# A weight sum by two chained transfers, and a residual sum by ScalarE copies and accumulating transfers

## The chip, the cores and the metric

The kernel runs on one core of one Trainium2 chip. The metric is the device time of one execution in microseconds. A core has five engines that each take their instructions in a fixed order: TensorE (PE; its weight loads are listed as PEld), VectorE (DVE), ScalarE (ACT), GpSimd (POOL) and SyncE (SP). SP issues most of the transfers (DMA), and POOL, too, can issue them.

## The reference

One encoder layer on x of 1024 tokens by 1024 columns, all in float32. An attention and retention part adds to x first. What matters here is the last part, the feed-forward one with 2816 hidden columns:

```
h2 = rmsnorm(x, norm2_w)
x = x + (silu(h2 @ w_gate) * (h2 @ w_up)) @ w_down
```

## The kernel before, in words

Every matrix product is made of three matmuls: each factor is split into a high part (rounded for PE) and a low part (what is missing), and high times high, high times low and low times high are summed in PSUM. For weights ACT writes the high part (`whi`) and DVE the low part (`wlo`); each of these two has two buffers in turn.

The tokens are worked in two halves of four blocks of 128. The first half's feed-forward part is plain. In the second half (`ffn_fast`) the gate and up products are made with 7 block products in place of 8 (a scheme after Winograd and Strassen). The hidden columns are worked in 11 pairs of 128-column tiles, and the pairs in groups: `self.groups` holds five groups of two pairs and a last one of one pair. For each pair the two weight matrices are cut in four quarters, q[0] to q[3], called quads: rows 0 to 511 or 512 to 1023 (c) and the first or second 128 columns of the pair (r). One quad holds the gate and the up part, 128 partitions by 1024 values. The seven weight factors m = 0 to 6 are made in `factor`:

- m = 0, 1 and 6 are q[0], q[1] and q[3] themselves
- m = 2 is s2 = s1 - q[0], with s1 = q[2] + q[3]; m = 3 is s1
- m = 4 is s3 = q[0] - q[2]; m = 5 is q[1] - s2, written over s2

The tiles s1, s2 and s3 take turns in a ring of two buffers (tag S), the quads in a ring of six. `chunk_parts` makes the high and low parts of two factors at a time; a pair of whi and wlo buffers holds two factors. `gate_up` runs PE over the seven products of a pair (24 matmuls each, 256 columns) and then the silu chain: ACT's tanh, three DVE instructions, ACT's write of the high part (Thi in the profile) and DVE's write of the low part (Tlo).

After a group's pairs comes `down`: for each of two column halves c of w_down (a chunk) and each of two pairs of token blocks, PE sums the products in two PSUM banks of 512 columns; six such banks take turns. DVE adds each bank to its residual tile `self.x1[b][c]`. In the last group the sum then goes to the output.

The tiles of tag wraw, three in turn, take the raw quarters of w_down and, ahead of this part, the normalised rows of x.

The order on each engine is set when the program is built. A planner in the kernel (`charge`, `tick`, `step`) estimates costs and due times and puts the preparation of later weights between matmuls; the build may then put an instruction ahead of earlier ones of its engine that are not ready yet by its own reckoning. In the profile nearly all instructions have line 99, that of the helper that records them, so groups are told apart by tile names: `S<-quad` is s1 or s3, `S<-S,quad` is s2, `S<-quad,S` is m = 5, `x<-d,x` a residual add, `u<-d` and `p<-d` are copies out of PSUM.

Of the kernel before, what the change touches and what calls it, by code (L numbers as in the profile page):

```python
# [10 lines left out]
AF = mybir.ActivationFunctionType  # L11
OP = mybir.AluOpType
# [3 lines left out]
S, D = 1024, 1024  # L16
# [6 lines left out]
NH = FFN // 128  # L23
# [95 lines left out]
class Layer:  # L119
# [14 lines left out]
    def new(self, pool, shape, dt, tag, bufs):  # L134

        t = pool.tile(shape, dt, tag=tag, name=tag, bufs=bufs)
        ring = self.rings.setdefault(tag, [])
        ring.append(t[:].tensor.name)
        if len(ring) > bufs:
            self.written[ring[-1]] = [(0, 1 << 30, self.touched.get(ring[-1 - bufs], 0.0), "")]  # L140
        return t
# [184 lines left out]
    def factor(self, pr, m):  # L326

        nc = self.nc
        q = self.quad(pr, 4)
        if m == 0:  # L330
            self.quad(pr + 1, 2)
        new = lambda: self.st([128, 2, 4, 128], tag="S", bufs=2)
        add = lambda out, a, b, op: nc.vector.tensor_tensor(out, a, b, op=op)
        if m == 2:
            self.s1, self.s2 = new(), new()
            add(self.s1, q[2], q[3], OP.add)
            add(self.s2, self.s1, q[0], OP.subtract)
            return self.s2
        if m == 3:
            return self.s1  # L340
        if m == 4:
            s3 = new()
            add(s3, q[0], q[2], OP.subtract)
            return s3
        if m == 5:
            add(self.s2, q[1], self.s2, OP.subtract)
            return self.s2
        return q[{0: 0, 1: 1, 6: 3}[m]]

    def chunk_parts(self, items):  # L350
        nc = self.nc
        hi, lo = [t[:, :1024 * len(items)].rearrange("p (i u k n) -> p i u k n", u=2, k=4, n=128) for t in self.wpair()]

        def fill():
            late = None
            for i, (pr, m) in enumerate(items):
                if late:
                    late()
                src = self.factor(pr, m)
                nc.scalar.activation(hi[:, i], src, AF.Copy)  # L360
                late = lambda i=i, src=src: nc.vector.tensor_tensor(lo[:, i], src, hi[:, i].bitcast(F32), op=OP.subtract)
                if m in (5, 6):
                    self.quad(pr + 1, m - 2)
                yield
            late()
        return (hi, lo), fill()
# [851 lines left out]
    def down(self, half, j0, g, hh, hl):  # L1218
        nc = self.nc
        for c in range(2):  # L1220
            hi, lo = self.weights()
            for t0 in (0, 2):
                ps = [self.pd(), self.pd()]
                for js in (range(g - 1), range(g - 1, g)):
                    for i in range(2):
                        ts = slice(128 * (t0 + i), 128 * (t0 + i) + 128)
                        for j in js:
                            nc.tensor.matmul(ps[i], hh[:, j, ts], hi[:, j, :], start=(j == 0), stop=False)
                            nc.tensor.matmul(ps[i], hh[:, j, ts], lo[:, j, :], start=False, stop=False)
                            nc.tensor.matmul(ps[i], hl[:, j, ts], hi[:, j, :], start=False, stop=(j == g - 1))  # L1230
                            self.tick()
                self.evacuate()
                for i in range(2):
                    b = 4 * half + t0 + i
                    xs = self.x1[b][c]
                    nc.vector.tensor_tensor(xs, ps[i], xs, op=OP.add)
                    if j0 == self.groups[-1][0]:
                        nc.scalar.dma_start(self.out[0, b * 128:(b + 1) * 128, 512 * c:512 * c + 512], xs)
# [115 lines left out]
```

## Time and profile before

| | us |
|---|---|
| median of 3 runs | 1301.08 |
| lowest and highest run | 1300.11, 1301.93 |
| the profiled execution | 1298.79 |
| its span | 1297.0 |
| PE busy in the span | 1258.3 |
| DVE busy | 1004.1 |
| ACT busy | 782.2 |
| POOL busy | 58.2 |

The span is what the profiler saw of the execution, from first to last instruction; the execution's own time has 1.79 us around it. An engine's busy time is the time in which it has an instruction under way. An idle time says nothing by itself: what counts is who waits for whom.

### The profile page before, as it was taken

What the parts mean: (1) busy time and instruction counts of PE and PEld (TensorE: products, weight loads), DVE (VectorE), ACT (ScalarE), POOL (GpSimd) and SP (SyncE); (2) the same over time, 40 slices, a digit from 0 to 9 for tenths busy, and PEclk for the clock granted to TensorE, in tenths of its full rate; (3) what the DMA queues carried; (4) which work ended last, traced back from release to release, by engine and by line L of the source; (5) the groups of instructions that cost most, each with busy time, mean ns of one, the idle gap of its engine ahead of it and who ended that gap; (6) DMA issues with size and microseconds to landing.
All of it is one profiled execution on the core that took longest, in us unless ns stands there. A gap on an engine that the chain in (4) does not pass through costs nothing.

```text
span 1297.0 us, 22620 instructions
## 1 busy us (share of the span) xinstructions
PE 1258.3 (97%) x8363; PEld 1131.0 (87%) x8363; DVE 1004.1 (77%) x2600; ACT 782.2 (60%) x1732; POOL 58.2 (4%) x68
## 2 busy tenths in 40 slices
PE   8799998999999999999999999999979999999998
PEld 7799898999999887888888878888969999898987
DVE  6679899888978877878787795645598787776866
ACT  7778976655695788468658944433355454443533
POOL 1401011010020000000000000000000000000000
PEclk8999999999999999999999999999989999999999
DMA  8433214221242222222223232225434242423311
GB/s 277 151 83 94 63 45 114 67 74 42 66 127 86 63 85 81 83 65 81 82 66 98 65 86 77 66 77 202 128 104 140 66 131 71 124 84 113 98 49 65
DMA packets 157790, 121.32 MB, mean 94 GB/s; under 512 B 8176, under 2 KB 137840, under 8 KB 157552
## 3 DMA queue, kind: packets, MB, share of 16 engines
q1 hardware_dynamic: 151744, 111.14, 29.1%
q10 hardware_dynamic: 5936, 8.74, 2.0%
q8 instruction: 65, 1.06, 0.3%
q14 instruction: 45, 0.37, 0.1%
HBM read 115.67 MB, written 4.19 MB: 92 GB/s over the span
## 4 chain that ended last, share of the span: by engine, by line
PE 70%; DVE 14%; ACT 10%; issue 3%; POOL 2%; DMA 1%; SPq 0%; ACTq 0%; POOLq 0%; DVEq 0%
PE d L99 60%; PE t L99 8%; ACT junk L99 4%; DVE wlo L99 2%; PE l L99 2%; DVE L L99 2%; ACT whi L99 2%; ACT Thi L99 1%; DMA bias<-in_near_dram 1%; DVE tr L99 0%; DVE cc L99 0%; DVE junk L99 0%; DVE maA L99 0%; DVE zqk L99 0%; POOL rc L99 0%
## 5 line engine op out<-in xcount | busy, mean ns | idle before, releaser
L99 PE MATMUL d<-whi,Thi 128*128 128x256 f32 (+2 forms) x1136 | 352.6, 311 | 5.5 <-ACT Thi L99 3.6
L99 PE MATMUL d<-wlo,Thi 128*128 128x256 f32 (+2 forms) x1136 | 342.7, 302 | 1.5 <-DVE wlo L99 1.4
L99 PE MATMUL d<-whi,Tlo 128*128 128x256 f32 (+2 forms) x1136 | 342.5, 302 | 0.0
L99 PEld LDWEIGHTS d<-whi,Thi 128*128 128x128 f32 x1136 | 216.0, 190 | 19.4 <-ACT Thi L99 5.9
L99 PEld LDWEIGHTS d<-wlo,Thi 128*128 128x128 f32 x1136 | 216.5, 191 | 10.3 <-DVE wlo L99 2.3
L99 PEld LDWEIGHTS d<-whi,Tlo 128*128 128x128 f32 x1136 | 215.9, 190 | 9.5 <-DVE Tlo L99 1.6
L99 ACT ACTIVATE whi<-wraw 128x512 fp32r<-128x512 f32 (+1 forms) x300 | 171.7, 616 | 69.4 <-PE d L99 55.5
L99 DVE TENSOR_TENSOR wlo<-wraw,whi 128x512 fp32r<-128x512 f32 (+1 forms) x302 | 197.3, 674 | 5.4 <-ACT whi L99 4.3
L99 ACT ACTIVATE junk<-sc,tc 128x384 bf16<-128x384 f32 (+5 forms) x186 | 163.6, 879 | 34.5 <-DVE tc L99 30.7
L99 PE MATMUL d<-Phi,whi 128*128 128x256 f32 x616 | 171.7, 279 | 8.1 <-ACT Phi L99 7.9
L99 PE MATMUL d<-Plo,whi 128*128 128x256 f32 x616 | 171.0, 278 | 0.0
L99 PE MATMUL d<-Phi,wlo 128*128 128x256 f32 x616 | 170.8, 277 | 0.0
L99 PE MATMUL d<-Thi,whi 128*128 128x512 f32 (+1 forms) x368 | 143.3, 390 | 0.0
L99 PE MATMUL d<-Tlo,whi 128*128 128x512 f32 (+1 forms) x368 | 141.9, 386 | 0.1
L99 PE MATMUL d<-Thi,wlo 128*128 128x512 f32 (+1 forms) x368 | 141.8, 385 | 0.0
L99 PEld LDWEIGHTS d<-Phi,whi 128*128 128x128 f32 x616 | 116.4, 189 | 9.2 <-ACT Phi L99 9.0
L99 PEld LDWEIGHTS d<-Plo,whi 128*128 128x128 f32 x616 | 116.2, 189 | 0.4 <-DVE Plo L99 0.2
L99 PEld LDWEIGHTS d<-Phi,wlo 128*128 128x128 f32 x616 | 116.2, 189 | 0.0
L99 DVE TENSOR_TENSOR x<-d,x 128x512 f32<-128x512 f32 (+1 forms) x64 | 39.1, 623 | 61.4 <-PE d L99 53.5
L99 ACT ACTIVATE whi<-S 128x1024 fp32r<-128x1024 f32 x44 | 45.4, 1054 | 67.6 <-PE d L99 57.3
L99 PEld LDWEIGHTS d<-Thi,wlo 128*128 128x128 f32 x368 | 69.1, 188 | 15.1
L99 PEld LDWEIGHTS d<-Tlo,whi 128*128 128x128 f32 x368 | 69.2, 188 | 12.7 <-DVE Tlo L99 0.4
(325 smaller groups left out, 2344.3 us busy)
## 6 DMA issues: line engine op xcount, KB each, us to landing
wraw<-in_w_down_dram SPq DMA_DIRECT2D x44, 512.0 KB, 3.8
wraw<-in_w_in_dram SPq DMA_DIRECT2D x24, 512.0 KB, 3.8
wraw<-in_w_gate_dram SPq DMA_DIRECT2D x44, 256.0 KB, 3.1
wraw<-in_w_up_dram SPq DMA_DIRECT2D x44, 256.0 KB, 3.5
quad<-in_w_gate_dram SPq DMA_DIRECT2D x44, 256.0 KB, 3.2
quad<-in_w_up_dram SPq DMA_DIRECT2D x44, 256.0 KB, 4.1
wraw<-in_w_in_dram SPq DMA_DIRECT2D x32, 256.0 KB, 3.4
wraw<-in_w_out_dram SPq DMA_DIRECT2D x16, 512.0 KB, 3.7
```

The costliest lines, as they stand in the source:

```text
L99: return f(*args, **kw)
```

## The change

Two parts, both in the second half.

First, DVE no longer makes s1. A new function `summed` loads q[2]'s rows and columns once more, straight into the tile of s1 (two transfers from SP, gate and up), and then has two transfers from POOL add q[3]'s rows and columns to it. For the first pair it is called when m = 0 is made, for a later one when m = 6 of the pair before is made. The quads are still loaded, since m = 4 and m = 6 use them.

Second, in `down` of the second half, in all groups but the last, ACT copies a bank to half of a tile of tag wraw, and a transfer from POOL adds that to the residual tile.

```
@@ factor @@
+        if (pr, m) == (0, 0):
+            self.summed(0)
         add = lambda out, a, b, op: nc.vector.tensor_tensor(out, a, b, op=op)
         if m == 2:
-            self.s1, self.s2 = new(), new()
-            add(self.s1, q[2], q[3], OP.add)
+            self.s1, self.s2 = self.s1, new()
             add(self.s2, self.s1, q[0], OP.subtract)
             return self.s2
...
+    def summed(self, pr):
+
+        if pr == NH // 2:
+            return
+        self.s1 = self.st([128, 2, 4, 128], tag="S", bufs=2)
+        for c, queue, kw in ((0, self.nc.sync, {}), (1, self.nc.gpsimd, {"accum_op": OP.add})):
+            for u, w in enumerate((self.w_gate, self.w_up)):
+                queue.dma_start(self.s1[:, u], w[512 * c:512 * c + 512, 256 * pr + 128:256 * pr + 256]
+                                .rearrange("(k p) n -> p k n", p=128), **kw)
...
@@ chunk_parts @@
                 if m in (5, 6):
                     self.quad(pr + 1, m - 2)
+                if m == 6:
+                    self.summed(pr + 1)
...
@@ down @@
                     xs = self.x1[b][c]
+                    if half and j0 < self.groups[-1][0]:
+                        if i == 0:
+                            tmp = self.sb([128, 1024], tag="wraw", bufs=3)
+                        ti = tmp[:, 512 * i:512 * i + 512]
+                        nc.scalar.activation(ti, ps[i], AF.Copy)
+                        nc.gpsimd.dma_start(xs, ti, accum_op=OP.add)
+                        continue
                     nc.vector.tensor_tensor(xs, ps[i], xs, op=OP.add)
```

## Rows read from the trace of the kernel before

**Rows 1.** The page's busy time of each engine, share of the span, instructions.
```profile
PE 1258.3 (97%) x8363; PEld 1131.0 (87%) x8363; DVE 1004.1 (77%) x2600; ACT 782.2 (60%) x1732; POOL 58.2 (4%) x68
```

**Rows 2.** Busy time of each engine (x instructions) in stretches, clock, DMA share, GB/s.
```profile
965.00:1280.00 315.00, 314.79 (x2251) 290.76 (x2251) 242.67 (x289) 146.89 (x207) 0.00 (x0) 1.00 0.31 91
...
1022.00:1032.00 10.00, 10.00 (x90) 10.00 (x89) 7.20 (x7) 5.70 (x7) 0.00 (x0) 1.00 0.59 158
1032.00:1042.00 10.00, 10.00 (x90) 10.00 (x89) 9.79 (x12) 5.94 (x8) 0.00 (x0) 1.00 0.29 84
```

**Rows 3.** Who waited for whom from 965 to 1280: total us, times, longest us.
```profile
ACT whi L99 <- PE d L99: 125.7, 41, 9.2
...
DVE S L99 <- DMA quad<-in_w_up_dram: 10.0, 5, 2.5
...
PEld d L99 <- ACT Thi L99: 1.8, 6, 0.7
PEld d L99 <- DVE Tlo L99: 1.6, 7, 0.3
...
PE d L99 <- ACT Thi L99: 0.2, 1, 0.2
```

**Rows 4.** The chain that ended last: start us, us, what.
```profile
961.51 149.28 PE d L99 x1102
...
1117.94 161.51 PE d L99 x1113
```

**Rows 5.** Stretches of 5 us ahead of 961, columns as in rows 2.
```profile
915.00:920.00 5.00, 5.00 (x45) 5.00 (x44) 0.84 (x2) 2.08 (x4) 0.00 (x0) 1.00 1.21 291
...
945.00:950.00 5.00, 0.00 (x0) 0.00 (x0) 5.00 (x10) 3.02 (x7) 0.00 (x0) 0.69 0.35 105
```

**Rows 6.** Timeline of DVE and SP: start us, us, instruction, [idle before <-releaser].
```profile
919.59 1.23 DVE L99 TENSOR_TENSOR S<-quad 128x1024 f32<-128x1024 f32 x1 [4.09 <-DMA quad<-in_w_up_dram]
...
917.57 1.11 SPq L99 DMA_DIRECT2D quad<-in_w_up_dram  x1
...
1022.47 0.50 SPq L99 DMA_DIRECT2D quad<-in_w_up_dram  x1
```

**Rows 7.** Groups by form from 965 to 1297: busy us, mean ns, idle before.
```profile
L99 DVE TENSOR_TENSOR x<-d,x 128x512 f32<-128x512 f32 x48 | 32.5, 691 | 47.5 <-PE d L99 47.4
...
L99 DVE TENSOR_TENSOR S<-quad 128x1024 f32<-128x1024 f32 x20 | 24.4, 1221 | 10.1 <-DMA quad<-in_w_up_dram 10.0
...
L99 ACT ACTIVATE u<-d 128x512 f32<-128x512 f32 x22 | 13.0, 590 | 8.1 <-PE d L99 8.1
```

**Rows 8.** Timeline of DVE in the second group, pairs 2 and 3.
```profile
1024.08 2.36 DVE L99 TENSOR_TENSOR wlo<-S,whi 128x1024 fp32r<-128x1024 f32 x2 [0.26 <-ACT whi L99]
...
1046.25 1.22 DVE L99 TENSOR_TENSOR wlo<-S,whi 128x1024 fp32r<-128x1024 f32 x1
...
1049.66 1.22 DVE L99 TENSOR_TENSOR S<-S,quad 128x1024 f32<-128x1024 f32 x1
...
1061.01 0.69 DVE L99 SCALAR_TENSOR_TENSOR Tlo<-th,Thi 128x512 fp32r<-128x512 f32 x1
```

**Rows 9.** Timeline of ACT, pairs 2 to 4.
```profile
1028.42 1.06 ACT L99 ACTIVATE whi<-quad 128x1024 fp32r<-128x1024 f32 x1 [2.06 <-PE d L99]
...
1033.82 1.06 ACT L99 ACTIVATE whi<-quad 128x1024 fp32r<-128x1024 f32 x1 [2.01 <-PE d L99]
...
1078.26 2.01 ACT L99 ACTIVATE whi<-S 128x1024 fp32r<-128x1024 f32 x2 [9.19 <-PE d L99]
```

**Rows 10.** Transfers: count, KB each, median us to landing; last line: all quads.
```profile
quad<-in_w_up_dram SPq DMA_DIRECT2D x44, 256.0 KB, 4.1
...
out_dram<-x ACTq DMA_DIRECT2D x8, 256.0 KB, 2.1
...
DMA to landing us min/median/max: 2.8/3.7/7.1
```

## The prediction

> **What bounds the kernel now.** I read the page's busy table first: TensorE (PE) is busy 97% of the span, VectorE (DVE) 77% [rows 1]. An average over stages says little about one stage, so next came the stretches. The change acts only from about 905 us on, in the feed-forward part of the second half. From 965 to 1280 us PE is busy 314.79 of 315.00 us, DVE 242.67, ScalarE (ACT) 146.89, GpSimd (POOL) 0.00 [rows 2]. Inside it, DVE is busy 9.79 of 10 us in one stretch and 7.20 in another; PE runs 90 matmuls in both [rows 2]. So a filled DVE does not slow PE here. The list of waits of the same stretch says what PE could get back: 1.8 + 1.6 + 0.2 = 3.6 us, all of it for Thi and Tlo, the hidden activations that the down products start on [rows 3]. ACT, by contrast, waits for PE 125.7 us [rows 3]. The chain that ended last agrees: its two long pieces are PE alone, 149.28 and 161.51 us [rows 4].
>
> Only ahead of 961 us does PE stand still for long: 0.00 busy in 945 to 950, where DVE is busy 5.00 of 5 [rows 5]. Nothing that the change removes is done there: the first s1 add runs at 919.59, and DVE had already waited 4.09 us for its transfer [rows 6].
>
> **The change, part by part.**
>
> *Removed.* Eleven s1 adds (half of the instructions S<-quad) at 1.22 us are 13.4 us. Of the 48 wide residual adds the last group keeps 8; 40 at 0.69 us are 27.6 us [rows 7]. DVE loses 41 us of work, yet PE can gain at most the 3.6 us above. I put 1.5 us: the Tlo part nearly whole, the Thi part not, since ACT writes Thi.
>
> *Copies on ACT.* 40 copies out of PSUM; the nearest row is u<-d, the same shape, 0.59 us [rows 7]: 23.6 us beside 146.89 busy in 315. Each can stand in ACT's queue behind a whi copy that waits for PE, 125.7 us in 41 waits [rows 3]. What waits for the copy is a PSUM bank; there are six, two for each pair of token blocks, so PE is two pairs ahead before it feels one. I take nothing; without that cover it is about one copy, 0.6 us, for each of ten weight chunks.
>
> *Residual transfers.* 40 SBUF to SBUF accumulations of 256 KB from POOL's queue. Nobody reads the sums until the next group's down stage, two pairs of 7 products later (37.8 us at the 2.70 us worked out below). The tmp tiles take turns in the wraw ring of three, so w_down loads of the next group come after those transfers; their values too are needed only at that stage. A load of the same bytes takes 4.1 us [rows 10]. Price: nothing; without the cover, one such landing a group.
>
> *The sum s1 by two transfers in a row.* This is the step that can cost. Two new SP loads stand in SP's queue behind the quads and ahead of the next quads and w_down loads; two accumulations wait for them on POOL, which does nothing else here [rows 2]. One issue takes SP about 0.5 us [rows 6], and what follows on SP is needed a pair later. But s1 takes the buffer of the previous pair's s2, free only when that pair's m = 5 low part is written. Take pair 3, the second of its group: that is at 1024.08 + 2.36 = 1026.44 [rows 8]. Then two issues, 1.0; a load, 4.1 (median of the up quarter [rows 10]); an accumulation. No accumulation is in the trace: below, 2.1 us (the landing of out<-x, the shortest median); above, 7.1 us (the slowest quad) [rows 10]; the nearest row is the up quarter, the same bytes from the same matrix, so 4.1. s1 is there at 1026.44 + 1.0 + 4.1 + 4.1 = 1035.6; with both legs short (2.8 + 2.1) at 1032.3, with both long (7.1 + 7.1) at 1041.6.
>
> When is it due? PE releases ACT's whi copies at 1028.42 and 1033.82 [rows 9]; a buffer holds two products, so a product takes 2.70 us. PE begins product (2,6) at 1033.8, (3,0) at 1036.5, (3,1) at 1039.2, (3,2) at 1041.9. Product (3,2) needs s2 (1.22), its whi (1.06) and its wlo (1.22) [rows 7 to 9]: s1 is due at 1041.9 - 3.5 = 1038.4. The margin is 2.8 us, and -3.2 with both legs long. That holds for the data of (3,2) alone. DVE takes its instructions in a fixed order: while s2 waits, wlo of (3,0) and (3,1) stand still if they are behind it.
>
> In the pairs that open a group s1 would land at 1046.25 + 1.22 + 9.2 = 1056.7 [rows 8] (bounds 1053.4 to 1062.7). Its reader, whi<-S at 1078.26 [rows 9], is 20 us off. But s2 stood at 1049.66, ahead of the silu instructions that end with Tlo at 1061.01 + 0.69 = 1061.70 [rows 8], and PE waits for Tlo in seven places already [rows 3]. If s2 keeps a place ahead of that Tlo, PE waits with it. If the order now puts it behind, that stretch is two adds, 2.4 us, shorter on DVE. I take one more short wait, of the 1.6 / 7 = 0.23 us that Tlo's average [rows 3], in each of five openings: 1.2 us, bounds 0 and those of the first rival.
>
> *A rule beside that row.* The rows give 4.1 us for each leg [rows 10]. The Trainium skill, page "DMA: Bandwidth & Descriptors", section "Anatomy of one DMA", fits one GpSimd-issued transfer as 2.0 us plus its bytes at 436 GB/s, an estimate of 2.6 us for 256 KB; by it s1 of pair 3 would stand at 1034.1. The same page, section "Two DMAs through the same engine are not ordered", has the second transfer wait for the first one's semaphore: the legs add up, as I have them, which no row here can show.
>
> *The first pair.* Its loads come behind twelve quad transfers, in a stretch with a transfer share of 1.21 [rows 5]. The last quad is issued at 917.57 and takes 1.11 us of SP [rows 6]; s1 stands at about 918.7 + 1.0 + 8.2 = 927.9. DVE has slack there (0.84 busy of 5 [rows 5]). I take 0.5 us, bounds 0 and 3.
>
> *Sum.* -1.5 + 1.2 + 0.5 = +0.2 us. The profiled execution took 1298.79 us (1.79 more than its span of 1297.0); the median of the runs, 1301.08, is 2.29 above it. So 1299.0 by the profile, 1301.3 for the median.
>
> **The rivals.** (1) *DVE stands still behind s2.* For it: DVE's order lets s1 wait for quads, 10.0 us in five places [rows 3], so it counts on transfers earlier than they land; two in a row double that error. Against: those five waits cost PE nothing. Place and price: in five group openings s2 stands ahead of Tlo, near 1054, and s1 lands at 1056.7: 2.7 us each, 13.5 us, 1314.6. With both legs long, 8.7 us there and 3.2 in five pairs inside groups, 59 us. It decides from the point where an accumulation takes over 1.4 us (1056.7 - 4.1 = 1052.6), if s2 has that place. (2) *PE gets faster.* As a mechanism: with DVE freer, matmuls follow one another closer, or the new order of DVE's queue gives back part of the 5 us at 945. Against the first: 90 matmuls in 10 us with DVE at 7.20 and at 9.79 [rows 2]. For the second only luck speaks; with 4 us of it the time is 1297. Beside this stands a rule: the Trainium skill, page "Trainium Kernel Development and Optimization", section "Best Practices", judges the distance to the roof by the busy share of weight loads, not of matmuls. Weight loads are busy 290.76 of 315 us [rows 2], so by that rule up to 24 us are open; the count of 90 does not bear it out. (3) *ACT's copies hold PSUM banks*: 0.6 us for each of ten chunks, 6 us, 1307; ACT's free half of the stretch speaks against it. (4) *DVE isn't relieved where it is full*: s2 waits longer than s1 took. Then the time is that of the forecast or of the first rival.
>
> **How the numbers follow.** The runs shown reach from 1300.11 to 1301.93, so 0.2%, 2.6 us, is about what can be told from no change. Forecast: 0.47, 1301.3, its own range 1299 to 1303.7. Rival 1: 0.39, mostly 1304 to 1320. Rival 2: 0.09. Rival 3: 0.05. Rival 4 is shared by the first two. Faster 0.09, same 0.47, slower 0.44. The range 1298.5 to 1319 leaves out some 0.07 at either end: below it rival 2, above it rival 1 with transfers nearer their upper bound.
>
> **What would show it.** Right: PE from 965 to 1280 still busy over 99.5%, with waits under 5 us; an accumulation landing within 5 us; DVE waiting at s2 for a transfer without PE waiting for wlo or Tlo; DVE's busy time in that stretch down by some 38 us, ACT's up by 23. Wrong: PE waits for wlo or Tlo of 1 us or more once in each group, with DVE at S<-S,quad before them; or PE waits for a bank after ACT's copies; or the stretch ahead of 961 is shorter or longer by more than 2 us.

## The result and the profile after

The changed kernel takes 1373.93 us (median of four runs, 1372.70 to 1377.18); the kernel before took 1301.07 us beside it. The ratio is 1.0568, 95% interval 1.0551 to 1.0585: 72.9 us slower. The forecast was 1301.3 us with a range up to 1319.0, so the result lies far outside. The nearest case is the first rival with long transfers (59 us), and the runs below show a second loss that no case of the prediction held.

The page of the changed kernel, busy time first (answers to [rows 1]), then TensorE's granted clock in 40 slices of the span:

```profile
PE 1286.0 (94%) x8363; PEld 1154.1 (84%) x8363; DVE 963.0 (70%) x2549; ACT 804.6 (59%) x1772; POOL 122.3 (9%) x130
...
PEclk9999999999999999999999999998899898999999
```

The relief is there as worked out: DVE 1004.1 to 963.0, 41.1 us less; ACT 22.4 us more. PE runs the same 8363 matmuls, is busy 27.7 us longer, and its share of the span falls. Where it stands still, the list of waits from 900 us on tells (us in total, times, longest):

```profile
DVE S L99 <- DMA S<-in_w_up_dram: 40.1, 5, 10.0
...
DVE S L99 <- issue: 27.1, 4, 10.0
PE d L99 <- ACT Thi L99: 21.6, 6, 5.5
PE d L99 <- DVE wlo L99: 21.4, 4, 6.0
```

In [rows 3] PE waited 3.6 us in all for Thi and Tlo. Now it waits 21.6 us for Thi and 21.4 for wlo, four to six times each, and DVE waits 67 us in nine places at S. Both waits of PE have one picture in DVE's timeline. First the second pair of a group, then the end of a group:

```profile
1039.57 2.35 DVE L99 TENSOR_TENSOR wlo<-S,whi 128x1024 fp32r<-128x1024 f32 x2
...
1047.76 0.68 DVE L99 TENSOR_TENSOR cc<-u,p 128x512 f32<-128x512 f32 x1
1058.47 1.23 DVE L99 TENSOR_TENSOR S<-S,quad 128x1024 f32<-128x1024 f32 x1 [10.04 <-DMA S<-in_w_up_dram]
...
1060.22 1.21 DVE L99 TENSOR_TENSOR wlo<-quad,whi 128x1024 fp32r<-128x1024 f32 x1
...
1085.24 1.23 DVE L99 TENSOR_TENSOR S<-S,quad 128x1024 f32<-128x1024 f32 x1 [5.70 <-issue]
1086.38 0.69 DVE L99 SCALAR_TENSOR_TENSOR th<-th,cc 128x512 f32<-128x512 f32 x1
...
1088.92 0.68 DVE L99 SCALAR_TENSOR_TENSOR Tlo<-th,Thi 128x512 fp32r<-128x512 f32 x1
```

S<-S,quad is s2. It stands in DVE's queue directly behind cc of the pair before, and DVE stands with it 10.04 us until the second transfer of s1 has landed. Behind it wait instructions that need nothing from it: the low part of product 1 (wlo<-quad, 1060.22) and, at a group's end, the tanh steps that lead to Thi and Tlo. (The releaser "issue" at 1085.24 says only that the trace shows none. It is the same instruction of another pair: the second transfer of its s1 was issued at 1077.10 and took 7.96 us to land, to 1085.06.) PE's timeline has the answer to both:

```profile
1055.16 0.28 PE L99 MATMUL d<-Plo,whi 128*128 128x256 f32 x1
1061.49 0.58 PE L99 MATMUL d<-Phi,wlo 128*128 128x256 f32 x1 [6.05 <-DVE wlo L99]
...
1082.64 0.39 PE L99 MATMUL d<-whi,Thi 128*128 128x512 f32 x1
1088.51 0.80 PE L99 MATMUL d<-whi,Thi 128*128 128x512 f32 x1 [5.48 <-ACT Thi L99]
```

The stand is not all that PE loses. Busy time by stretches (columns as in [rows 2]): the long stretch, then ahead of the pause, in it, just after it, and later:

```profile
965.00:1280.00 315.00, 275.48 (x1824) 252.62 (x1825) 166.65 (x196) 138.57 (x202) 48.84 (x48) 0.92 0.62 138
...
1050.00:1055.00 5.00, 5.00 (x46) 5.00 (x46) 0.00 (x0) 0.75 (x1) 2.62 (x2) 1.00 1.26 265
1056.00:1061.00 5.00, 0.00 (x0) 0.00 (x0) 2.52 (x3) 0.67 (x2) 0.00 (x0) 0.78 0.23 29
1061.50:1065.50 4.00, 4.00 (x19) 4.00 (x20) 4.00 (x6) 2.47 (x4) 0.00 (x0) 0.50 0.00 0
1066.00:1071.00 5.00, 4.48 (x38) 4.29 (x37) 5.00 (x7) 3.24 (x6) 0.00 (x0) 1.00 0.63 184
```

Ahead of the pause PE runs 46 matmuls in 5 us at a granted clock of 1.00 (2.4 GHz). In the pause the clock falls, and in the 4 us behind it 0.50 is granted (1.2 GHz): 19 matmuls where the earlier rate would give 37. The same 0.50 stands in the 4 us from 1088.55, 1213.85, 1240.95 and 1291.70, each behind another pause. So a pause is paid for again after it has ended.

The account, from the starts of PE's matmuls: the distance between two starts is 0.113 us for 256 columns and 0.2335 for 512 when nothing disturbs. An excess over 0.9 us counts as a pause, all others together as slow matmuls. It begins in both kernels with the 6002nd matmul (954.76 before, 958.99 after). Before: pauses 3.80, slow 4.03. After: pauses 49.25, slow 28.08, of which 23.4 lie within 8 us behind a pause. The differences are 45.45 us of pauses and 24.05 of slow matmuls. With the 4.23 us by which the 6002nd already starts later they make the 73.73 us by which the last one does (1292.89 and 1366.62).

The list of transfers (count, KB each, median us to landing) answers to [rows 10]:

```profile
quad<-in_w_up_dram SPq DMA_DIRECT2D x44, 256.0 KB, 5.0
...
S<-in_w_up_dram SPq DMA_DIRECT2D x11, 256.0 KB, 5.4
S<-in_w_gate_dram POOLq DMA_DIRECT2D x11, 256.0 KB, 4.7
S<-in_w_up_dram POOLq DMA_DIRECT2D x11, 256.0 KB, 6.8
```

The second leg of s1 lands after 6.8 us, not 4.1. And on SP's queue and POOL, around the pair above:

```profile
1001.96 40.10 SPq L99 DMA_DIRECT2D wraw<-in_w_down_dram  x4
...
1044.27 1.59 SPq L99 DMA_DIRECT2D S<-in_w_gate_dram  x1
...
1051.10 1.30 POOL L99 DMA_DIRECT2D S<-in_w_gate_dram  x1 [16.27 <-DMA S<-in_w_gate_dram]
1051.98 1.73 POOL L99 DMA_DIRECT2D S<-in_w_up_dram  x1
```

SP stands at four w_down loads for 40.10 us, to 1042.06. The loads of quads and of s1 are behind them. In [rows 6, 8] a quad of this pair was issued at 1022.47, ahead of the low parts at 1024.08; here the quads come after the same low parts (1039.57).

### The profile page after: what moved, and what is told of

Same layout as the page of the kernel before. It is cut to its first block, busy times and chain, and to the rows that moved or that the text cites. A ratio compares the mean times of both kernels' runs of the same rounds, so it can differ in the third digit from the quotient of the medians.

```text
span 1370.9 us, 22842 instructions
## 1 busy us (share of the span) xinstructions
PE 1286.0 (94%) x8363; PEld 1154.1 (84%) x8363; DVE 963.0 (70%) x2549; ACT 804.6 (59%) x1772; POOL 122.3 (9%) x130
## 5 line engine op out<-in xcount | busy, mean ns | idle before, releaser
L99 PE MATMUL d<-whi,Thi 128*128 128x256 f32 (+2 forms) x1136 | 356.4, 314 | 24.1 <-ACT Thi L99 21.6
L99 PE MATMUL d<-Phi,wlo 128*128 128x256 f32 x616 | 178.2, 289 | 21.4 <-DVE wlo L99 21.4
L99 PE MATMUL d<-Phi,whi 128*128 128x256 f32 x616 | 178.4, 290 | 11.3 <-ACT Phi L99 7.4
L99 PE MATMUL d<-Plo,whi 128*128 128x256 f32 x616 | 177.3, 288 | 0.0
L99 PEld LDWEIGHTS d<-Phi,wlo 128*128 128x128 f32 x616 | 122.4, 199 | 22.2 <-DVE wlo L99 22.2
L99 PEld LDWEIGHTS d<-Phi,whi 128*128 128x128 f32 x616 | 122.5, 199 | 13.7 <-ACT Phi L99 8.4
L99 PEld LDWEIGHTS d<-Plo,whi 128*128 128x128 f32 x616 | 122.0, 198 | 0.4 <-DVE Plo L99 0.2
L99 DVE TENSOR_TENSOR wlo<-S,whi 128x1024 fp32r<-128x1024 f32 x44 | 52.8, 1219 | 45.0 <-ACT whi L99 45.0
L99 DVE TENSOR_TENSOR wlo<-quad,whi 128x1024 fp32r<-128x1024 f32 x33 | 39.9, 1223 | 56.6 <-ACT whi L99 56.6
```

Of the source, the lines that this page charges most:

```text
L99: return f(*args, **kw)
```

## The experiments

Times are medians; the ratio is to the kernel before, run beside each, with its 95% interval. The first four put two questions: which part costs, and is it DVE's stand or the transfers.

**The sum alone** (residual adds left on DVE):

```diff
-                    if half and j0 < self.groups[-1][0]:
-                        ...
-                        nc.gpsimd.dma_start(xs, ti, accum_op=OP.add)
-                        continue
                     nc.vector.tensor_tensor(xs, ps[i], xs, op=OP.add)
```

> Only the weight sum by transfers; the residual stays with DVE adds. Theory W (DVE stands at s2 until the second transfer of s1 has landed, and everything behind it in DVE's queue with it): nearly all of the loss is here, 1350 to 1374 us, with a PE wait of 4 to 6 us in each pair from the second on. Rival Q (the tmp tiles hold up the w_down loads in SP's queue, and these hold up the quads and the loads of s1): without tmp tiles the loads are early, 1301 to 1320.

1365.33 us, ratio 1.0503 (1.0470 to 1.0535): 64 us. Waits, and the timeline of DVE and SP, of this kernel:

```profile
DVE S L99 <- DMA S<-in_w_up_dram: 27.5, 5, 6.1
...
PE d L99 <- ACT Thi L99: 19.6, 5, 5.0
DVE S L99 <- DMA wraw<-in_w_down_dram: 19.2, 4, 5.2
...
PE d L99 <- DVE wlo L99: 8.6, 4, 2.3
```

The third line names w_down, but it is s2 again: in all four places it starts 0.17 or 0.18 us after the second transfer of s1 has landed (at 1084.66 us and 1084.84, for one).

```profile
1042.75 2.36 DVE L99 TENSOR_TENSOR wlo<-S,whi 128x1024 fp32r<-128x1024 f32 x2 [0.26 <-ACT whi L99]
...
1044.01 0.37 SPq L99 DMA_DIRECT2D S<-in_w_gate_dram  x1
...
1057.52 1.23 DVE L99 TENSOR_TENSOR S<-S,quad 128x1024 f32<-128x1024 f32 x1 [6.06 <-DMA S<-in_w_up_dram]
```

The first load of s1 is issued at 1044.01, as soon as the first of the two low parts is written: that one frees the buffer. From there to s2 (1057.52) it is 13.5 us. The prediction had 9.2 for the same way, and counted from the second low part.

**The residual alone** (s1 added on DVE as before):

```diff
-        if (pr, m) == (0, 0):
-            self.summed(0)
...
-            self.s1, self.s2 = self.s1, new()
+            self.s1, self.s2 = new(), new()
+            add(self.s1, q[2], q[3], OP.add)
...
-                if m == 6:
-                    self.summed(pr + 1)
```

> Only the residual by ACT copies and accumulating transfers; s1 stays with DVE. Theory W: 1299 to 1304, no PE wait over 1 us after 962 us. Rival Q: the quads come late behind w_down loads, 1310 to 1340. Rival B (ACT copies hold PSUM banks): 1305 to 1310 with PE waits in the down stages.

1318.64 us, ratio 1.0137 (1.0114 to 1.0161): 17.4 us where I had priced nothing. What SP waited for most from 990 to 1300 us, then SP's queue and DVE, of this kernel:

```profile
SPq L99 <- DMA x<-wraw: 152.8, 18, 20.3
```

```profile
1011.97 14.91 SPq L99 DMA_DIRECT2D wraw<-in_w_down_dram  x3
...
1035.47 1.23 DVE L99 TENSOR_TENSOR S<-quad 128x1024 f32<-128x1024 f32 x1 [8.45 <-DMA quad<-in_w_up_dram]
```

The w_down loads take turns in the ring with the copies that ACT makes, so a load waits on SP for a copy's transfer (x<-wraw) to end, and the quads stand behind it. The kernel before has no such transfer. DVE waits 8.45 us at s1 where it waited 2.5 at most in [rows 3].

**The whole change, s2 made by GpSimd:**

```diff
-            add(self.s2, self.s1, q[0], OP.subtract)
+            nc.gpsimd.tensor_tensor(self.s2, self.s1, q[0], op=OP.subtract)
```

> The changed kernel, but s2 = s1 - q[0] is made by POOL in place of DVE, so that DVE never stands at it. Theory W: the waits for Thi at the group ends go (5 x 5.6 us and the slow clock after them), what stays is that the factor itself is late in the second pair of a group: 1315 to 1340. If DVE's standing is not the cause: 1365 to 1380.

1364.82 us, ratio 1.0477 (1.0460 to 1.0495). The expectation failed; the stand had moved to the next engine that takes its work in order:

```profile
ACT whi L99 <- POOL S L99: 41.6, 5, 10.1
PE d L99 <- ACT p L99: 37.6, 5, 9.3
```

ACT's copy whi of s2 now stands ahead of the copies p that free PE's banks. The run takes s2 off DVE, but not out of an in-order queue, and so does not tell place from lateness.

**The whole change, with one leg:** no accumulation; DVE adds the last quarter to s1.

```diff
+            add(self.s1, self.s1, q[3], OP.add)
...
-        for c, queue, kw in ((0, self.nc.sync, {}), (1, self.nc.gpsimd, {"accum_op": OP.add})):
+        for c, queue, kw in ((0, self.nc.sync, {}),):
```

> The changed kernel without the accumulating transfers of s1: q[2] is loaded into its tile by SP as in the change, and DVE adds q[3] to it before it makes s2. Theory W with the second leg as the main part (6 to 8 us from POOL's issue to its end): s1 stands about when the quads do, 1300 to 1312. If the first leg, behind the quads and after the wait for the ring, is already late: 1330 to 1360.

1339.72 us, ratio 1.0298 (1.0282 to 1.0313): the accumulation is worth 34 us of the 72.9, but not all.

**The residual with tiles of its own.** The copies go to tiles that hold PE's products (p1, u2, u3, p5) instead of the w_down ring; on top of the residual alone:

```diff
-                        if i == 0:
-                            tmp = self.sb([128, 1024], tag="wraw", bufs=3)
-                        ti = tmp[:, 512 * i:512 * i + 512]
+                        ti = self.st([128, 512], tag=("p1", "u2", "u3", "p5")[t0 + i])
```

> Only the residual part, with its copies in tiles that stand empty in the down stage (p1, u2, u3, p5) and not in the ring of the w_down loads. Theory Q (the 17 us of the residual part alone come from w_down loads that wait in SP's queue for those transfers, with quads behind them): the four PE waits of 2.5 to 4.2 us go, 1299 to 1303. If the accumulating transfers themselves or ACT's copies cost it: 1314 to 1320.

1301.96 us over 11 runs against 1300.37 over 15, ratio 1.0009 (1.0000 to 1.0018). Of 17.4 us 1.6 stay. SP and DVE of this kernel:

```profile
1000.19 2.77 SPq L99 DMA_DIRECT2D wraw<-in_w_down_dram  x2
...
1027.94 0.39 SPq L99 DMA_DIRECT2D quad<-in_w_up_dram  x1
...
1031.74 1.23 DVE L99 TENSOR_TENSOR S<-quad 128x1024 f32<-128x1024 f32 x1 [2.76 <-DMA quad<-in_w_up_dram]
```

The same 40 copies and 40 transfers, but SP is done with the w_down loads at 1002.96, 25 us ahead of the quad shown: the residual part's cost was the shared ring and SP's queue. It also tells what 27.6 us less on DVE are worth here when the copies and transfers that replace them add no wait: no time.

**The sum alone, first leg alone** (DVE adds the last quarter; no residual part): the edit of the one-leg run on the sum alone.

> Only the weight sum, and of it only the load of q[2] by SP; DVE adds q[3] and subtracts q[0]. Theory W with the second leg as the larger part of the 64 us: 1310 to 1325, DVE waiting 2 to 4 us for the load in each pair. If the first leg is as much: 1330 to 1345.

1325.02 us, ratio 1.0192 (1.0177 to 1.0207): 24.7 us. The second leg costs the other 40 of the sum's 64 us.

**A control, and an earlier start.** The control is the kernel before with five quad buffers instead of six. The second kernel is the sum alone; it has five too, gives s1 a buffer of its own, and calls the sum at product 4 instead of 6:

```diff
-            q = self.st([128, 2, 4, 128], tag="quad", bufs=6)
+            q = self.st([128, 2, 4, 128], tag="quad", bufs=5)
...
-        self.s1 = self.st([128, 2, 4, 128], tag="S", bufs=2)
+        self.s1 = self.st([128, 2, 4, 128], tag="S1", bufs=1)
...
-                if m == 6:
+                if m == 4:
                     self.summed(pr + 1)
```

> Control for the next run: the kernel before with five quad buffers in place of six. 1301 to 1310; quads come somewhat later. Both theories expect the same.

> Only the weight sum, with a buffer of its own for s1 (paid for with one quad buffer), called at m = 4 and so free after m = 3's low part: both transfers start some 6 us earlier and ahead of the next quads in SP's queue. Theory W (lateness of s1 is the whole cost): within 10 us of the control with five quads. If the transfers cost by their traffic or on POOL rather than by lateness: 1345 to 1370, as with the weight sum alone.

The control: 1311.98 us, ratio 1.0089 (1.0074 to 1.0105). The early start: 1349.44, ratio 1.0379 (1.0359 to 1.0399), 37.5 us over the control where I expected at most 10. DVE of the early start:

```profile
1043.73 1.23 DVE L99 TENSOR_TENSOR S<-S,quad 128x1024 f32<-128x1024 f32 x1 [4.72 <-issue]
1046.01 2.35 DVE L99 TENSOR_TENSOR wlo<-quad,whi 128x1024 fp32r<-128x1024 f32 x2
```

With s1 earlier, s2 has moved forward too, ahead of low parts that stood before it, and DVE again stands some 5 us. So my theory that s1 starts too late fell. What was left: s2 gets a place in DVE's queue a few us ahead of the landing, wherever the landing is.

**s2 fixed behind the low part of product 1.** One edge that orders two instructions on DVE; the edit touches no buffer and no transfer. On the sum alone:

```diff
-                late = lambda i=i, src=src: nc.vector.tensor_tensor(lo[:, i], src, hi[:, i].bitcast(F32), op=OP.subtract)
+                late = lambda i=i, src=src: setattr(self, "low", nc.vector.tensor_tensor(
+                    lo[:, i], src, hi[:, i].bitcast(F32), op=OP.subtract))
...
-            add(self.s2, self.s1, q[0], OP.subtract)
+            with self.tc.issue_after(self.low.ins):
+                add(self.s2, self.s1, q[0], OP.subtract)
```

> The sum part alone (residual adds on DVE as before), with one order fixed by hand: s2's subtraction may not stand in DVE's queue ahead of the low part of product 1 of its own pair. The transfers are untouched: same queues, same buffers, same starts. Theory P (the cost of the sum part is the place of s2 in DVE's in-order queue, some 5 us ahead of the landing of the accumulation, with the low part of product 1, the tanh steps and Tlo queued behind it): the waits of PE for Thi at the group ends (5.0 us each, about 20 us) and for the low part of product 1 (8.6 us) go, and most of the 28.8 us of slow matmuls with them; of the 64 us 15 to 60 go: 1305 to 1350, my value 1320, since in the middle of a group product 2 itself may still come 1 to 3 us late. Rival L (product 2 is late whatever stands ahead of it, since the accumulation lands too late for PE): PE waits as long, for the low part of product 2 in place of product 1's: 1355 to 1370. Rival T (the transfers themselves slow the rest): 1355 to 1370, with waits for quads or w_down loads.

1310.33 us, ratio 1.0066 (1.0052 to 1.0080): of 64 us 9 stay. The stretch of [rows 2], the waits, and DVE's timeline at a group's end and in the pair after it:

```profile
965.00:1280.00 315.00, 311.43 (x2183) 285.48 (x2182) 229.80 (x274) 142.45 (x202) 25.99 (x20) 1.00 0.52 125
```

```profile
DVE S L99 <- DMA S<-in_w_up_dram: 7.1, 5, 1.9
...
PE d L99 <- ACT p L99: 2.9, 4, 0.9
PE d L99 <- ACT Thi L99: 1.3, 1, 1.3
...
PE d L99 <- DVE wlo L99: 0.2, 1, 0.2
```

```profile
1075.26 1.22 DVE L99 TENSOR_TENSOR S<-S,quad 128x1024 f32<-128x1024 f32 x1
...
1100.40 1.23 DVE L99 TENSOR_TENSOR wlo<-quad,whi 128x1024 fp32r<-128x1024 f32 x1 [0.29 <-ACT whi L99]
1103.76 1.23 DVE L99 TENSOR_TENSOR S<-S,quad 128x1024 f32<-128x1024 f32 x1 [1.53 <-DMA S<-in_w_up_dram]
```

At the group's end s2 runs without a wait; inside the group it waits 1.53 us with the low part of product 1 already written, and PE is busy 311.43 of 315 us at a clock of 1.00. The transfers land as late: from the first load of s1 (1090.82) to s2 it is 12.9 us here, against 13.5 in the sum alone. What cost was the place of s2. Counted as in the account above, slow matmuls are 21.7 us more than before in the sum alone and 6.6 here.

**The same with the early start:**

> The kernel with the sum started at product 4 into a buffer of its own and five quad buffers (1349.4, against a control with five quad buffers at 1312.0), with the same order fixed: s2 behind the low part of product 1. Theory P: the two together leave nothing that is late; within 8 us of the control, 1304 to 1320. Rival L or T: most of the 37 us stays, 1335 to 1350.

1303.51 us (10 runs), ratio 1.0015 (1.0004 to 1.0027), and so below its control of 1.0089. In none of the eleven pairs does s2 wait for its transfers. Why it beats the control was not followed; five quad buffers made DVE wait for quads there, and this kernel's s1 needs no quads.

**The whole change with s2 fixed, and with both mends** (s2 fixed and the residual's own tiles):

> The whole change with s2 fixed behind the low part of product 1; the residual copies still take turns with the w_down loads. Theory P: the sum part's share falls away, and what stays is the residual part's 17 us through SP's queue: between 1315 and 1345. Rivals L and T: 1360 to 1375.

> The whole change with both mends: s2 behind the low part of product 1, and the residual copies in tiles of their own, so that no w_down load waits for them. Theory P with the finding on SP's queue: 1298 to 1325, at or a little above the result of the sum part alone with the same order, since the residual part in tiles of its own cost about 1 us. Not faster than the kernel before by more than 3 us, since PE computes without a gap there. Rivals L and T: 1350 to 1370.

1330.49 us, ratio 1.0218 (1.0202 to 1.0233), and 1309.25 us, ratio 1.0061 (1.0048 to 1.0074). The first of them, on SP and DVE:

```profile
1014.82 15.22 SPq L99 DMA_DIRECT2D wraw<-in_w_down_dram  x3
...
1046.42 1.23 DVE L99 TENSOR_TENSOR S<-S,quad 128x1024 f32<-128x1024 f32 x1 [6.28 <-DMA S<-in_w_up_dram]
```

Here the place is right and s1 itself comes late, behind SP's stand at w_down. The ring costs 21.2 us (1330.49 - 1309.25), as it cost 15.8 without the sum (17.4 - 1.6).

## Why the prediction was wrong, point by point

*"Residual transfers ... Price: nothing."* This step failed, with 17.4 us by itself. It asked when the values of w_down are needed, not what stands behind their loads on SP. The prediction itself says that the loads come after those transfers in a ring of three; the next line on that queue, the quads, is needed within a few us. Shown by the pair of runs that differ in the tiles alone (17.4 and 1.6 us).

*"If the order now puts it behind ... I take one more short wait ... in each of five openings: 1.2 us."* This step failed most. s2 kept a place ahead of the tanh steps, and PE stood at the groups' ends: 5.48 us in the one shown, 21.6 us for Thi in all. The first rival had this mechanism and both its places, openings and inner pairs; I gave it 0.39. Shown by the edge that moves s2 alone (64 to 9 us).

*The leg at 4.1 us.* Mis-sized: an accumulation takes 4.7 us for the gate half and 6.8 for the up half, which ends last, and POOL is busy 1.30 to 1.73 us issuing one. From a free buffer to s2 it is 13.5 us in the sum alone, not 9.2. That is inside the bounds (1.0 + 7.1 + 7.1), but the margin of 2.8 us for pair 3 is gone. By the Trainium skill, page "DMA: Bandwidth & Descriptors", section "Anatomy of one DMA", the estimate was 2.6 us; these 22 accumulations disagree, and the measurement decides. By the Trainium skill, same page, section "Two DMAs through the same engine are not ordered", the issuing engine has to wait for the first transfer's semaphore. The trace agrees: POOL waited for the first leg (16.27 us at 1051.10) before it issued the second.

*The sum's unit.* Even with the right waits the sum would have been short: it had no term for the granted clock. Behind pauses of some 5 us the clock stood at 0.50 for about 4 us; 24 of the 73.7 us are slow matmuls. The 59 us of the first rival had none either.

*Range.* It ended at 1319.0, below the 1360 that the first rival gave with both legs long, and it had no case for SP's queue.

*The parts are not additive.* 64.1 and 17.4 make 81.5, the change costs 72.9. Both delay the same landing; that this is the reason was not shown.

*What held.* PE was the bound, and DVE's relief gives no time: with 27.6 us taken off DVE and no wait added the time is the same within 0.2%. DVE's busy time fell by 41.1 us (41 worked out), ACT is busy 22.4 us longer (23.6), and no wait of PE names one of its new copies. The second rival's rule, the Trainium skill, page "Trainium Kernel Development and Optimization", section "Best Practices", by which up to 24 us were open in the share of weight loads, is not borne out by these runs: no relieved kernel came below the one before.

*The first pair.* Priced at 0.5 us, at most 3; this term, too, was mis-sized. On DVE, and in the list of PE's waits:

```profile
930.83 1.23 DVE L99 TENSOR_TENSOR S<-S,quad 128x1024 f32<-128x1024 f32 x1 [10.00 <-issue]
```

```profile
PE t L99 <- DVE wraw L99: 3.6, 1, 3.6
```

s2 stood 10.00 us, until just after the second transfer landed (930.75). The normalised rows of x (wraw), which PE transposes, come behind it on DVE, and PE waited 3.6 us for one. From the 5601st matmul to the 6002nd it took 61.1 us, against 56.2 before and 56.6 with s2 fixed: some 5 us.

*What stays open.* The sum alone keeps 9.0 us with its order mended. In its profile the last matmul starts 9.5 us later than before: 1.7 in pauses, 6.6 in slow matmuls, 1.2 ahead of the 6002nd. I did not follow them further. That the order of DVE's queue rests on an expected landing that comes too early is argued from the early start, where the place moved along with the transfer; the runs show the place and its price, not how it is chosen. No version ran faster than the kernel before; the nearest are the residual in tiles of its own (1.0009) and the early sum with s2 fixed (1.0015).

## What to carry to other kernels

Work that goes from a full engine to a transfer leaves a wait in an in-order queue. Before pricing the data's lateness, name the place of its first reader in that queue and every instruction behind it that needs nothing from it; if the reader can be put behind those, the same late transfer is nearly free (64 us to 9 here). A buffer ring shared by loads and by tiles that a slow transfer still has to read puts that transfer's time into the load queue, and everything behind the load pays, even if that load itself is early. And where TensorE is saturated, a pause of 5 us costs more than 5 (here 45 us of pauses came with 24 us of slow matmuls).

## What the runs showed of the hardware

- Behind pauses of about 5 us TensorE was granted 0.50 of its clock for some 4 us (1061.50 to 1065.50), 1.00 again from 1066; before, 1.00 all through the stretch.
- An accumulating transfer of 256 KB from POOL's queue took 4.7 and 6.8 us to land beside plain loads at 5.0 and 5.4, and POOL 1.30 to 1.73 us to issue.
- A load that waits for its buffer holds its whole queue: 40.10 us on SP for four w_down loads.
